# The low part of a weight quarter made by ScalarE and an adding transfer, and high products ahead of low ones

## The chip, the cores and the metric

The program runs on one core of a Trainium2 chip. The metric is the device time of one execution in microseconds (us), from the first instruction to the last. Five engines work side by side, each through its own instruction queue in order: TensorE (PE: matmuls, with its weight loads shown as PEld), VectorE (DVE), ScalarE (ACT), GpSimd (POOL) and SyncE (SP, which here only issues transfers). Transfers from the chip's memory (DRAM) to the on-chip buffer run on 16 DMA engines and are issued from the queues of SP, ACT or POOL.

## The reference

One backbone layer over 256 latent tokens and 256 context tokens of width 2048, in float32:

```python
h  = modulate(rmsnorm(x, norm1_w), sh1, sc1);  hc = the same for ctx
rw, cv, z, ab, gt = split(h @ w_in);  rw_c, ... = split(hc @ w_in)
out_a = prefix_scan(rwkv7_scan, ...)       # 16 heads of 64, two directions, context first
out_b = prefix_scan(gdn_chunked, ...)      # 8 heads of 128, two directions, context first
y = (sigmoid(g_a) * (o_a @ p_a) + sigmoid(g_b) * (o_b @ p_b)) @ w_out
x = x + gt1 * y
x = x + gt2 * swiglu(modulate(rmsnorm(x, norm2_w), sh2, sc2), w_gate_up, w_down)
return rmsnorm(x, final_norm_w)
```

Every large product (`h @ w_in`, the merges, `w_out`, the FFN) has to be close to float32.

## The kernel before

**Split products.** TensorE is given float32 numbers rounded to a shorter form (F32R). A weight block is therefore split: `hi = round(raw)`, `lo = raw - hi`; the activations are kept split in the same way (`HX`, `HC`: a high and a low tile of the latent and of the context tokens). A product is three matmuls per 128 rows of weights: hi with high, hi with low, lo with high.

**Blocks and quarters.** A block of `w_in` is 2048 by 128, that is 16 slices of 128 by 128. It is loaded, split and used in four quarters of four slices (`CG = 4`; a quarter is 128 x 512 numbers, 256 KB), numbered q = 0 to 3. A block for both token groups (what = k, v, K, V) takes 24 matmuls a quarter, two-sided; one for the latent tokens alone (r, Q, and g, the 40 gate blocks) takes 12, one-sided. There are 86 blocks of `w_in` in this part, 31 two-sided and 55 one-sided. Blocks of the merge matrices `pa` and `pb` have at most two quarters.

**What a quarter passes through.** `fetch` takes a raw buffer from the ring `raws` (three buffers at first, up to six later) and has SP issue the load. `cast` waits for the landing, takes a slot of the ring `his` and has ScalarE write `hi`; takes a slot of `los` and has VectorE write `lo`; gives the raw buffer back; and marks the quarter as cast. `products` runs the matmuls and gives the slots of `his` and `los` back after the quarter's last one. Both rings have four slots, so a quarter's cast can start only when the quarter four before it, the same q of the block before, is used up.

**The order of the work.** From about 100 us to 1330 us of the span a planner (`Weave`) weaves many generators together: the products, which fill TensorE whenever nothing of higher rank is ready, and the chains of the two scans (`prepare`, `grams`, `inverse`, `scan`, then `features`, `decays`, `head_grams`, `head_inverse`, `head_scan`). Each yields operations with an estimated cost (`LAT` holds the constants); the planner picks whichever can start first and so writes out a fixed order for each of TensorE, VectorE, ScalarE and GpSimd. On the chip every engine keeps that order, whatever the real times are. SP issues the loads as the plan asks for them. All operations of the woven part have line 164 in the profile, where a helper records them (SP's loads have line 175, preloads of activation tables line 154). After it come the last merges and `w_out` (L1861, L1862), and the FFN (L426, L427, L436 to L438), which use other code.

Of the kernel before, what the change touches and what calls it, by code (L numbers as in the profile page):

```python
# [11 lines left out]
F32 = mybir.dt.float32  # L12
F32R = mybir.dt.float32r
AF = mybir.ActivationFunctionType
ALU = mybir.AluOpType
# [3 lines left out]
P = 128  # L19
D = 2048  # L20
KT = D // P
T = 256
# [5 lines left out]
NHELD, NB = 10, 10  # L28
GATES_A, GATES_B = ((36,0,0,0,0,0,0,0),(0,0,0,0,0,4,0,0))

LAT = dict(dma=3.1, v=1.0, s=1.0, hop=dict(e=0.215, v=0.135, s=0.15, g=0.1), slack=0.1, own=0.09, grp=32, crank=-1, cg=4, into=0.14, back=0.2, cross=0.14, stay=0.0, gpace=1.6)
LNEXP = "natural_log_exp_and_others"
SIGM = "sigmoid_and_others"
UNIT = 64 * 64 + 64
# [78 lines left out]
class Lane:  # L113
# [36 lines left out]
    def __getattr__(self, name):  # L150

        def op(out, *a, **k):
            if name == "preload_act_table_set":
                return Op(self, 1.2, lambda: self.engine.preload_act_table_set(out))
            if name == "dma_start":
                return Op(self, 0.6 if self.each > 0.002 else 0.06, lambda: self.engine.dma_start(out, *a))
            mode = base = None
            if name == "transpose" and len(a) == 2:
                cost, mode = 0.109, "full"
            elif name == "matmul":  # L160
                cost, mode = self.product(out, a)
            else:
                cost, base = self.cost(name, out, a, k), (out.offset // out.ap[0][0], out.shape[0])
            return Op(self, cost, lambda: getattr(self.engine, name)(out, *a, **k), mode, base)  # L164
        return op
# [163 lines left out]
def emit(ctx: ExitStack, tc, A, out, dbg=None):  # L329
# [4 lines left out]
    weave = Weave()  # L334
    dq = Loads(Q)
    e, v, s, g = (Lane(x, fixed, each, LAT["own"], LAT["hop"][n]) for x, fixed, each, n in
                  ((E, 0.0, 0.0, "e"), (V, 0.07, 0.00104, "v"), (S, 0.06, 0.0009, "s"), (G, 0.06, 0.0022, "g")))
# [137 lines left out]
    with tc.tile_pool(name="p0", bufs=1) as p0, \  # L475
# [12 lines left out]
        low = [pst(pi, "pi"), pst(pmm, "mm"), pst(psq, "s"), pst(psq, "s"), pst(pmm, "mm"), pst(pa, "pa")]  # L488
# [23 lines left out]
        ps = pst(pa, "pa")  # L512
# [71 lines left out]
        for part in range(NE + 1):  # L584
            if part < NE:
                ps = pst(pmm, "mm")
            for c in range(4):
# [4 lines left out]
                if c == 0 and part < NE:  # L592
                    w = low_split(part)
# [197 lines left out]
    CG = LAT['cg']  # L791
# [5 lines left out]
    raws, his, los = quarters("wraw", 3, F32), Ring(quarters("whi", 2, F32R)), Ring(quarters("wlo", 2, F32R))  # L797
# [366 lines left out]
    def cast(parts, i):  # L1164

        for q, part in enumerate(parts):
            n = part.shape[1]
            yield "asked", i, q
            raw, at = landed.pop((i, q))
            yield max(0.0, at - weave.now)  # L1170
            hi = yield his
            yield s.copy(hi[:, :n], raw[:, :n])
            lo = yield los
            yield v.tensor_sub(lo[:, :n], raw[:, :n], hi[:, :n].bitcast(F32))
            raws.put(raw)
            casts[i, q] = hi, lo
            weave.ready("cast", i, q)

    def weights(parts, i):
        weave.add(LAT['crank'], fetch(parts, i))  # L1180
# [74 lines left out]
    def products():  # L1255
# [53 lines left out]
        while todo or ahead:  # L1309
            ask(1)  # L1310
            if not ahead:
                yield 0.5
                continue
            what, p, need = ahead.pop(0)
            ask(NQ)
            if need is not None:
                yield need
            if what == "l":
                yield "cast", i, 0
                hi, lo = casts.pop((i, 0))  # L1320
                yield "part", NGH - 1
                for j in range(p, min(p + CG, NHELD)):
                    for n, (w, part) in enumerate(((hi, 0), (hi, 1), (lo, 0))):
                        yield e.matmul(held[j // 2][:, T * (j % 2):T * (j % 2) + T], w[:, j - p], OB[part][:, NGH - 1, :],
                                       start=False, stop=j % 2 == 1 and n == 2)
                    if j % 2:
                        weave.add(150, second_merge(j - 1, 2, held[j // 2], homes[j // 2]))
                his.put(hi)
                los.put(lo)
                i += 1  # L1330
                continue
            if what != "b":
                ps = yield mmb
            elif p % 2 == 0:
                if p >= 6:
                    yield "inv", NGH - 1
                held.append((yield homes[p // 2]))
            if what in "bf":
                nk = NGH - (what == "b")
                half = p % 2 if what == "b" else 0  # L1340
                for k in range(nk):
                    if k % CG == 0:
                        ask(NQ, k == CG)
                        yield "cast", i, k // CG
                        hi, lo = casts.pop((i, k // CG))
                    yield "part", k
                    for j, (w, part) in enumerate(((hi, 0), (hi, 1), (lo, 0))):
                        yield e.matmul((held[-1] if what == "b" else ps)[:, T * half:T * half + T], w[:, k % CG], OB[part][:, k, :],
                                       start=k + j + half == 0, stop=what == "f" and k == nk - 1 and j == 2)
                    if k in (CG - 1, nk - 1):  # L1350
                        his.put(hi)
                        los.put(lo)
                i += 1
                if what == "f":
                    weave.add(150, second_merge(p, 1, ps))
                continue
            sides = ((0, OA),) if what == "p" else ((0, HX), (1, HC))[:1 + (what in "kvKV")]
            nk = OA[0].shape[1] if what == "p" else KT
            for k in range(nk):
                if k % CG == 0:  # L1360
                    ask(NQ, k == nk - CG)
                    yield "cast", i, k // CG
                    hi, lo = casts.pop((i, k // CG))
                for j, (w, part) in enumerate(((hi, 0), (hi, 1), (lo, 0))):
                    for a, X in sides:
                        yield e.matmul(ps[:, T * a:T * a + T], w[:, k % CG], X[part][:, k, :], start=k + j + a == 0,
                                       stop=k == nk - 1 and j == 2 and a == len(sides) - 1)
                if k % CG == CG - 1:
                    his.put(hi)
                    los.put(lo)  # L1370
            i += 1
            if what not in NPARTS and not any(x[0] not in NPARTS for x in todo + ahead):
                weave.ready("sides")
            if what == "g":
                weave.add(150, gate_out(rs, p, ps))
            elif what == "p":
                weave.add(150, first_merge(p, ps, p == KT - 1))
            else:
                (hd if what in "KVQ" else pr)[p][what + "ps"] = ps
                weave.ready(what + "gemm", p)  # L1380
# [713 lines left out]
```

## Time and profile before

| what | us |
|---|---|
| median of 3 runs | 2189.1 (2182.12 to 2189.5) |
| the profiled execution, its own time | 2182.99 |
| its span, first to last instruction | 2181.2 |
| PE busy in the span | 2104.2 |
| DVE busy in the span | 1551.6 |
| ACT busy in the span | 1119.0 |
| POOL busy in the span | 19.3 |

A busy PE counts the whole modelled time of a matmul, and matmuls overlap in a pipeline, so a short wait between two of them can hide in its share. In the rows, "x" is a count, "<-" in a group is output from inputs, and "<-" behind an idle time names what ended it. The granted TensorE clock was 0.989 of full speed on the mean.

### The profile page before, as it was taken

Reading aid. Unit: us, or ns where it says so; the run is one execution under the profiler, and the core shown is the slowest. Engines: PE = TensorE matmul, PEld = TensorE weight load, DVE = VectorE, ACT = ScalarE, POOL = GpSimd, SP = SyncE. Lnnn points to the kernel's source line nnn. Section 1 sums busy time; section 2 is a strip of 40 time slices with the busy share of each in tenths; the row PEclk is TensorE's granted clock in tenths of the full one; section 3 lists DMA queues with packets and bytes.
Section 4 is the critical chain, followed back from the end, with each engine's and each line's share of the span. In section 5 each row is a group of like instructions: output and inputs, shape, how many; then the busy total and the mean of one; then the engine's idle time right before and its main releaser. Section 6 shows DMA issues by size and latency. Waiting matters only on the chain.

```text
span 2181.2 us, 59117 instructions
## 1 busy us (share of the span) xinstructions
PE 2104.2 (96%) x24536; PEld 1973.0 (90%) x24536; DVE 1551.6 (71%) x3305; ACT 1119.0 (51%) x2210; POOL 19.3 (1%) x55
## 2 busy tenths in 40 slices
PE   7999999999999999999999998999999999999997
PEld 4987698888898898998989988999999999999997
DVE  4466599889889976898998777865666665554554
ACT  3246654555555556565565664644444444444443
POOL 0000000000000000000000000000000000000000
PEclk9999999999999999999999999999999999999999
DMA  9966756645565564665653745946777776566665
GB/s 385 410 168 198 228 140 180 188 141 154 164 162 154 159 168 142 188 194 169 173 160 105 218 151 178 306 161 216 242 244 239 242 239 209 195 191 194 196 194 163
DMA packets 276813, 431.14 MB, mean 198 GB/s; under 512 B 119872, under 2 KB 137664, under 8 KB 272192
## 3 DMA queue, kind: packets, MB, share of 16 engines
q1 hardware_dynamic: 262720, 402.19, 60.0%
q10 hardware_dynamic: 13824, 25.17, 3.6%
q8 instruction: 192, 3.15, 0.6%
q14 instruction: 77, 0.63, 0.1%
HBM read 401.50 MB, written 25.77 MB: 196 GB/s over the span
## 4 chain that ended last, share of the span: by engine, by line
PE 80%; DVE 7%; DMA 7%; ACT 3%; issue 2%; SPq 1%; DVEq 0%; ACTq 0%
PE mm L164 27%; PE mm L438 12%; PE mm L437 12%; PE mm L436 12%; PE s L164 6%; PE pa L164 5%; PE pi L164 3%; DVE arena L164 2%; DMA wraw<-w 2%; DVE wlo L164 1%; DMA wraw<-ada_rest 1%; PE mm L529 1%; PE s L579 1%; PE mm L579 1%; ACT whi L164 1%
## 5 line engine op out<-in xcount | busy, mean ns | idle before, releaser
L427 DVE TENSOR_TENSOR wlo<-wraw,whi 128x1024 fp32r<-128x1024 f32 (+1 forms) x264 | 315.0, 1193 | 292.6 <-ACT whi L426 292.4
L426 ACT CAST whi<-wraw 128x1024 fp32r<-128x1024 f32 (+1 forms) x264 | 270.6, 1025 | 386.6 <-PE mm L437 341.7
L164 PE MATMUL mm<-hxh,wlo 128*128 128x256 f32 x1376 | 399.5, 290 | 7.0 <-DVE wlo L164 6.4
L164 PE MATMUL mm<-hxh,whi 128*128 128x256 f32 x1376 | 397.2, 289 | 2.8 <-ACT whi L164 1.8
L164 PE MATMUL mm<-hxl,whi 128*128 128x256 f32 x1376 | 395.7, 288 | 0.0
L438 PE MATMUL mm<-hfh,wlo 128*128 128x256 f32 x1344 | 371.7, 277 | 0.6 <-DVE wlo L427 0.6
L436 PE MATMUL mm<-hfh,whi 128*128 128x256 f32 x1344 | 371.0, 276 | 0.0
L437 PE MATMUL mm<-hfl,whi 128*128 128x256 f32 x1344 | 371.0, 276 | 0.0
L164 ACT CAST whi<-wraw 128x512 fp32r<-128x512 f32 (+1 forms) x399 | 243.1, 615 | 206.1 <-PE mm L164 93.5
L164 DVE TENSOR_TENSOR wlo<-wraw,whi 128x512 fp32r<-128x512 f32 (+1 forms) x399 | 270.4, 680 | 86.0 <-ACT whi L164 82.7
L164 PEld LDWEIGHTS mm<-hxh,wlo 128*128 128x128 f32 x1376 | 260.7, 189 | 17.9 <-DVE wlo L164 9.8
L164 PEld LDWEIGHTS mm<-hxh,whi 128*128 128x128 f32 x1376 | 260.7, 189 | 10.9 <-issue 4.1
L164 PEld LDWEIGHTS mm<-hxl,whi 128*128 128x128 f32 x1376 | 261.1, 190 | 6.5 <-issue 4.1
L438 PEld LDWEIGHTS mm<-hfh,wlo 128*128 128x128 f32 x1344 | 252.3, 188 | 1.1 <-DVE wlo L427 1.0
L437 PEld LDWEIGHTS mm<-hfl,whi 128*128 128x128 f32 x1344 | 252.3, 188 | 0.0
L436 PEld LDWEIGHTS mm<-hfh,whi 128*128 128x128 f32 x1344 | 252.3, 188 | 0.0
L164 PE MATMUL mm<-hch,wlo 128*128 128x256 f32 x496 | 142.3, 287 | 0.0
L164 PE MATMUL mm<-hcl,whi 128*128 128x256 f32 x496 | 142.2, 287 | 0.1
L438 PE MATMUL mm<-za,wlo 128*128 128x256 f32 x512 | 141.4, 276 | 0.1
L436 PE MATMUL mm<-za,whi 128*128 128x256 f32 x512 | 141.5, 276 | 0.0
L437 PE MATMUL mm<-za,whi 128*128 128x256 f32 x512 | 141.3, 276 | 0.0
L164 PE MATMUL mm<-hch,whi 128*128 128x256 f32 x496 | 140.9, 284 | 0.0
(417 smaller groups left out, 4519.8 us busy)
## 6 DMA issues: line engine op xcount, KB each, us to landing
wraw<-w SPq DMA_DIRECT2D x344, 256.0 KB, 3.3
wraw<-wgu SPq DMA_DIRECT2D x168, 512.0 KB, 4.7
aw<-ada_first SPq DMA_DIRECT2D x32, 1024.0 KB, 10.3
wraw<-wdn SPq DMA_DIRECT2D x64, 448.0 KB, 3.7
wraw<-ada_rest SPq DMA_DIRECT2D x96, 256.0 KB, 3.3
aw<-ada_rest SPq DMA_DIRECT2D x48, 512.0 KB, 4.3
wraw<-wout SPq DMA_DIRECT2D x64, 256.0 KB, 5.9
aw<-ada_gt ACTq DMA_DIRECT2D x64, 256.0 KB, 5.2
```

The source lines that it names most:

```text
L164: return Op(self, cost, lambda: getattr(self.engine, name)(out, *a, **k), mode, base)
L426: S.copy(hi[:, c, :M], raw[:, c, :M])
L427: V.tensor_sub(lo[:, c, :M], raw[:, c, :M], hi[:, c, :M].bitcast(F32))
L436: E.matmul(ps, hi, Xh[:, k, :n], start=first and i == 0, stop=False)
L437: E.matmul(ps, hi, Xl[:, k, :n], start=False, stop=False)
L438: E.matmul(ps, lo, Xh[:, k, :n], start=False, stop=last and i == len(wt) - 1)
L529: E.matmul(ps[32 * g:32 * g + 32, 0:P], ckr[:, k].rearrange("p a b -> p (a b)"), aws[e, c][:, i, g], start=k == 0, stop=k == KT - 1)
L579: E.matmul(ps[:m, T * a:T * a + T], w_, X[:, 2 * e + k, :], start=e == k == i == 0, stop=e == NE - 1 and k == 1 and i == len(todo) - 1)
```

## The change

In the woven part, for the blocks with four quarters:

- For the last quarter of each block (q = 3) the subtraction on VectorE goes. ScalarE, behind its cast, writes minus the high part into the low slot, and a transfer issued from GpSimd's queue reads the raw weights from DRAM a second time and adds them there. The raw buffer goes back as soon as the cast is issued.
- For every quarter of these blocks TensorE now runs the eight (one-sided) or sixteen (two-sided) products with `hi` first and then the four or eight with `lo`. The low part has a mark of its own ("low"), and only the low products wait for it. Products of `pb` keep their order and wait for both marks.
- The planner's costs get a time for the adding transfer (`acc=4.0`).

```diff
-LAT = dict(dma=3.1, v=1.0, s=1.0, ... gpace=1.6)
+LAT = dict(dma=3.1, v=1.0, s=1.0, ... gpace=1.6, acc=4.0, share=lambda i, q: q == 3)
...
-                return Op(self, 0.6 if self.each > 0.002 else 0.06, lambda: self.engine.dma_start(out, *a))
+                return Op(self, 0.6 if self.each > 0.002 else 0.06, lambda: self.engine.dma_start(out, *a, **k))
...
             yield s.copy(hi[:, :n], raw[:, :n])
             lo = yield los
-            yield v.tensor_sub(lo[:, :n], raw[:, :n], hi[:, :n].bitcast(F32))
-            raws.put(raw)
             casts[i, q] = hi, lo
-            weave.ready("cast", i, q)
+            if len(part.shape) == 3 and part.ap[-2][0] == P and LAT["share"](i, q):
+                raws.put(raw)
+                weave.ready("cast", i, q)
+                weave.add(LAT['crank'], low_part(part, lo[:, :n], hi[:, :n].bitcast(F32), i, q))
+            else:
+                weave.ready("cast", i, q)
+                yield v.tensor_sub(lo[:, :n], raw[:, :n], hi[:, :n].bitcast(F32))
+                raws.put(raw)
+                weave.ready("low", i, q)
+
+    def low_part(part, lo, hi, i, q):
+
+        yield s.activation(lo, hi, AF.Copy, scale=-1.0)
+        yield g.dma_start(lo, part, accum_op=ALU.add)
+        yield LAT["acc"]
+        weave.ready("low", i, q)
...
-                for j, (w, part) in enumerate(((hi, 0), (hi, 1), (lo, 0))):
+                for j, part in enumerate((0, 1)):
                     for a, X in sides:
-                        yield e.matmul(ps[:, T * a:T * a + T], w[:, k % CG], X[part][:, k, :], start=k + j + a == 0,
-                                       stop=k == nk - 1 and j == 2 and a == len(sides) - 1)
+                        yield e.matmul(ps[:, T * a:T * a + T], hi[:, k % CG], X[part][:, k, :], start=k + j + a == 0, stop=False)
                 if k % CG == CG - 1:
+                    yield "low", i, k // CG
+                    for kk in range(k - CG + 1, k + 1):
+                        for a, X in sides:
+                            yield e.matmul(ps[:, T * a:T * a + T], lo[:, kk % CG], X[0][:, kk, :], start=False,
+                                           stop=kk == nk - 1 and a == len(sides) - 1)
                     his.put(hi)
                     los.put(lo)
```

Because the planner's costs and marks change, it writes a new order for the whole woven part. Three places of it follow; a row is line, operation, output and inputs, shape, and a count.

The start of a quarter of a gate block on TensorE, before: each slice has its low product right behind its two high ones, and the quarter's first low product waits for VectorE.

```order
L164 MATMUL mm<-hxh,whi 128x256 [waits Activation_49]
L164 MATMUL mm<-hxl,whi 128x256
L164 MATMUL mm<-hxh,wlo 128x256 [waits DVE_49]
L164 MATMUL mm<-hxh,whi 128x256
L164 MATMUL mm<-hxl,whi 128x256
```

The end of a last quarter (q = 3) of such a block on TensorE, and the start of the block behind it, now:

```order
L164 MATMUL mm<-hxh,whi 128x256
L164 MATMUL mm<-hxl,whi 128x256
L164 MATMUL mm<-hxh,wlo 128x256 [waits DMASW2_49]
L164 MATMUL mm<-hxh,wlo 128x256 x3
L164 MATMUL mm<-hxh,whi 128x256 [waits Activation_49]
L164 MATMUL mm<-hch,whi 128x256
```

The four low products stand together behind the eight high ones and wait for a transfer of GpSimd's queue (DMASW) instead of VectorE; nothing else stands between the high and the low products here.

On GpSimd, in the second head pair (`prepare`: a memset of `ei`, the copy and the sum of `bon`, and the memsets of the next inverse), before:

```order
L896 MEMSET arena 128x8
L928 COPY bon<-arena 128x256
L900 MEMSET arena 128x8
L930 TENSOR_TENSOR bon<-bon,arena 128x256
L164 MEMSET arena 128x256
```

The same place now:

```order
L896 MEMSET arena 128x8
L156 DMA wlo<-w 128x512
L928 COPY bon<-arena 128x256
L900 MEMSET arena 128x8
L156 DMA wlo<-w 128x512
L930 TENSOR_TENSOR bon<-bon,arena 128x256
L156 DMA wlo<-w 128x512 x2
L164 MEMSET arena 128x256
```

Transfers (86 in all) now stand between and behind GpSimd's own instructions, some of which wait for VectorE.

On ScalarE, where the gates are turned into sigmoids (`gts<-gts`) near the end of the woven part and a head's readout (`arena<-s,C`: logarithm, then exponential) comes by, before:

```order
L164 ACTIVATE gts<-gts 128x512
L164 COPY PA<-mm 128x256
L164 CAST whi<-wraw 128x512
L154 ACT_TABLE_LOAD
L164 CAST whi<-wraw 128x512
L164 ACTIVATE arena<-arena 128x256
L164 COPY PA<-mm 128x256
L164 CAST whi<-wraw 128x512
L164 ACTIVATE arena<-s,C 128x256
```

And now:

```order
L164 ACT_TABLE_LOAD
L164 ACTIVATE arena<-s,C 128x256
L164 ACT_TABLE_LOAD
L164 ACTIVATE gts<-gts 128x512
L164 ACT_TABLE_LOAD
L164 ACTIVATE arena<-arena 128x256
L164 COPY PA<-mm 128x256
L164 ACT_TABLE_LOAD
L164 ACTIVATE gts<-gts 128x512
```

The readout has moved ahead of the last sigmoids and in between them, with four table loads around it. Over the whole program ScalarE has 39 table loads in its order where it had 34.

More of the change, by code (lines that the diff above doesn't have):

```diff
@@ L29 @@
 GATES_A, GATES_B = ((36,0,0,0,0,0,0,0),(0,0,0,0,0,4,0,0))
-LAT = dict(dma=3.1, v=1.0, s=1.0, hop=dict(e=0.215, v=0.135, s=0.15, g=0.1), slack=0.1, own=0.09, grp=32, crank=-1, cg=4, into=0.14, back=0.2, cross=0.14, stay=0.0, gpace=1.6)
+LAT = dict(dma=3.1, v=1.0, s=1.0, hop=dict(e=0.215, v=0.135, s=0.15, g=0.1), slack=0.1, own=0.09, grp=32, crank=-1, cg=4, into=0.14, back=0.2, cross=0.14, stay=0.0, gpace=1.6, acc=4.0, share=lambda i, q: q == 3)
 LNEXP = "natural_log_exp_and_others"
@@ L1319, in products @@
                 yield "cast", i, 0
+                yield "low", i, 0
                 hi, lo = casts.pop((i, 0))
@@ L1363, in products @@
                     hi, lo = casts.pop((i, k // CG))
-                for j, (w, part) in enumerate(((hi, 0), (hi, 1), (lo, 0))):
+                for j, part in enumerate((0, 1)):
                     for a, X in sides:
-                        yield e.matmul(ps[:, T * a:T * a + T], w[:, k % CG], X[part][:, k, :], start=k + j + a == 0,
-                                       stop=k == nk - 1 and j == 2 and a == len(sides) - 1)
+                        yield e.matmul(ps[:, T * a:T * a + T], hi[:, k % CG], X[part][:, k, :], start=k + j + a == 0, stop=False)
                 if k % CG == CG - 1:
+                    yield "low", i, k // CG
+                    for kk in range(k - CG + 1, k + 1):
+                        for a, X in sides:
+                            yield e.matmul(ps[:, T * a:T * a + T], lo[:, kk % CG], X[0][:, kk, :], start=False,
+                                           stop=kk == nk - 1 and a == len(sides) - 1)
                     his.put(hi)
```

## The prediction

> **What bounds the kernel now.** I read the page first, then the windows, the groups, the waits, and single stretches of the timeline and of the chain.
>
> The page's span, busy times and chain:
>
> ```profile
> span 2181.2 us, 59117 instructions
> PE 2104.2 (96%) x24536; PEld 1973.0 (90%) x24536; DVE 1551.6 (71%) x3305; ACT 1119.0 (51%) x2210; POOL 19.3 (1%) x55
> PE 80%; DVE 7%; DMA 7%; ACT 3%; issue 2%; SPq 1%; DVEq 0%; ACTq 0%
> ```
>
> TensorE carries four fifths of the chain that ended last; VectorE is on it for 7%, about 153 us, ScalarE for 3%, about 65 us. The windows show where the rest lies: first the woven part as a whole, then 100 us of it, then 100 us of the FFN (columns: window, its length, then busy us and count for PE, PEld, DVE, ACT, POOL, the granted clock, the DMA share, GB/s).
>
> ```profile
> 100.00:1330.00 1230.00, 1188.15 (x16140) 1079.44 (x16128) 1004.50 (x2481) 701.62 (x1628) 18.88 (x50) 0.99 0.59 171
> 300.00:400.00 100.00, 96.36 (x1386) 89.11 (x1384) 88.98 (x199) 54.47 (x136) 3.60 (x10) 1.00 0.63 176
> 1500.00:1600.00 100.00, 100.00 (x884) 100.00 (x883) 61.69 (x92) 44.19 (x55) 0.00 (x0) 1.00 0.76 244
> ```
>
> In the FFN TensorE is never idle. In the woven part it is idle for 1230 - 1188.15 = 41.9 us, and VectorE is busy for 82% of it, 89% in the quoted stretch. Only this part is touched. The groups give the prices:
>
> ```profile
> L164 PE MATMUL mm<-hxh,wlo 128*128 128x256 f32 x1376 | 399.5, 290 | 7.0 <-DVE wlo L164 6.4
> L438 PE MATMUL mm<-hfh,wlo 128*128 128x256 f32 x1344 | 371.7, 277 | 0.6 <-DVE wlo L427 0.6
> L164 DVE TENSOR_TENSOR wlo<-wraw,whi 128x512 fp32r<-128x512 f32 (+1 forms) x399 | 270.4, 680 | 86.0 <-ACT whi L164 82.7
> L164 ACT CAST whi<-wraw 128x512 fp32r<-128x512 f32 (+1 forms) x399 | 243.1, 615 | 206.1 <-PE mm L164 93.5
> L164 ACT ACTIVATE arena<-arena 128x512 f32<-128x512 f32 (+2 forms) x108 | 62.3, 585 | 24.2 <-DVE arena L164 19.7 <-issue 3.4
> L164 ACT ACT_TABLE_LOAD x14 | 18.0, 1283 | 0.2
> 1269.87 8.09 PE mm L164 x71
> ```
>
> The same product takes 290 ns in the woven part and 277 ns in the FFN; the 13 ns are short waits hidden in the pipeline. The last row, of the chain, is the pace of products that wait for nothing: 8.09 us for 71, or 0.114 us each. So a one-sided quarter (12 products) is 1.37 us of TensorE, a two-sided one 2.74. The waits that the change touches:
>
> ```profile
> PE mm L164 <- DVE wlo L164: 6.4, 13, 1.5
> PEld mm L164 <- DVE wlo L164: 9.8, 16, 1.7
> ACT whi L164 <- PE mm L164: 93.5, 66, 4.9
> SPq L175 <- DVE wlo L164: 226.4, 166, 6.9
> ACT whi L164 <- DMA wraw<-w: 68.5, 48, 3.2
> ```
>
> TensorE visibly waits for a low part for 6.4 us only (9.8 at its weight loads, the same waits seen one step earlier). Casts wait for a slot (ScalarE on TensorE, 93.5 us) more than for a load (68.5 us).
>
> **The change, part by part.**
>
> *The subtractions that go.* 86 x 0.680 = 58.5 us of VectorE, 5.8% of its 1004.5 us there. Only the time when VectorE is on the path counts. Most of the 153 us of chain on VectorE lies in the woven part; I take 130, and 5.8% of that is 7.5 us. The ends are 0 and 41.9 us (all idle time of TensorE); I take 8, because the idle time is spread over many releasers.
>
> *High products first.* The first low product moves from the third to the ninth place of a one-sided quarter, 6 x 0.114 = 0.7 us later, and from the fifth to the seventeenth of a two-sided one, 1.4 us later. The longest wait of 13 was 1.5 us, so nearly all 6.4 us go. Where the supply of casts is the limit the wait only moves to the next high part; hidden waits go too. I take 6, between 0 and 16 (6.4 + 9.8).
>
> *Raw buffers back earlier.* A quarter of SP's 226.4 us of waits for a subtraction are of last quarters, and their buffer comes back about 1 us sooner. A load that comes sooner helps where a cast waited for it, a quarter of 68.5 us at most; TensorE mostly did not wait for that. I take 2, between 0 and 17.
>
> *The adding transfer.* Nothing in the trace adds on its way, and nothing is issued by GpSimd's queue. The nearest rows (KB each, us from issue to landing) and the slots:
>
> ```profile
> wraw<-w SPq DMA_DIRECT2D x344, 256.0 KB, 3.3
> wraw<-wgu SPq DMA_DIRECT2D x168, 512.0 KB, 4.7
> sgd__1597<-lo ACTq DMA_DIRECT2D x32, 256.0 KB, 4.1
> 405.76 0.62 ACT L164 CAST whi<-wraw 128x512 fp32r<-128x512 f32 x1
> 406.41 0.69 DVE L164 TENSOR_TENSOR wlo<-wraw,whi 128x512 fp32r<-128x512 f32 x1 [0.38 <-PE pa L164]
> 1199.26 0.62 ACT L164 CAST whi<-wraw 128x512 fp32r<-128x512 f32 x1 [1.21 <-PE mm L164]
> 1201.08 0.62 ACT L164 CAST whi<-wraw 128x512 fp32r<-128x512 f32 x1 [1.20 <-PE mm L164]
> ```
>
> It must at least read 256 KB as a plain load does, 3.3 us; it reads the low tile as well, 512 KB together, 4.7 us; were it a load and then a write one behind the other, 3.3 + 4.1 = 7.4. I take 4.7, whose byte count it shares. The low part is then ready at: slot free, cast 0.62, minus high 0.6 (between the 585 and 615 ns rows), handovers (406.38 to 406.41 is 0.03) 0.1, transfer 4.7, and some 0.4 behind other work on ScalarE, which is busy 57% of the time (701.62 of 1230): 6.4 us. The ends are 5.0 and 9.1.
>
> Against it stands the time from the release of the slot (the last low product of the block before) to the first low product of this last quarter. With nothing between products that is three quarters and eight products: 44 x 0.114 = 5.0 us one-sided, 10.0 two-sided. Two-sided blocks are covered to the upper end. One-sided ones: the two cast rows at 1199.26 and 1201.08 are a stretch of Q blocks whose casts wait for slots, 1.82 us a quarter, so 3 x 1.82 + 0.9 = 6.4 us; and over the whole part the products of all 86 blocks (55 x 5.5 + 31 x 10.9 = 640 us) fill about 1100 us, so the mean is 5.0 x 1.7 = 8.6 us. A quarter of the 55, the gate blocks with little between them, I put below 6.4, short by 0.5 us on the mean: 14 x 0.5 = 7 us of waiting. At the lower end it is 0. At the upper end (9.1) some 40 blocks are short by 1.9 us: 76 us.
>
> The Trainium skill (DMA: Bandwidth & Descriptors, section "Anatomy of one DMA — SWDGE (gpsimd) path") gives a transfer issued from GpSimd as about 2.0 us plus the bytes at 436 GB/s, which is an estimate of 2.6 us for 256 KB without the adding. No run here shows such a transfer, and SP's plain load took 3.3 us. By that page the low part would be ready in 4.3 us, the 7 us would be 0 and the sum -10, or 2173, still inside the forecast's own range.
>
> *ScalarE.* 86 x 0.6 = 52 us for minus high, and five more table loads (39 against 34 in the order) at 1.283: 6.4 us, together 58 us on 701.6, 8.3%. Cover: ScalarE's 43% of idle time. Of its 65 us on the chain some 45 lie in the woven part; 8.3% is 4 us. Four of the loads fall into the stretch of sigmoids, in front of casts that feed TensorE; the four slots hold 5.5 us of one-sided products, so I add only 1. Total 5, between 0 and 58.
>
> *DMA.* 22.5 MB more are read and as much is read back from the low tiles, in a part whose engines are 59% busy; q1's 402 MB take 60% of the whole span, so 45 MB are about 7% of it, or 12% of the woven part. Engines stay under 75%; loads that meet an adding transfer land a little later. I take 1, between 0 and 10.
>
> *GpSimd's queue.* 86 issues on an engine that is busy 18.9 of 1230 us: 0, as long as its own instructions do not hold the transfers up (a rival).
>
> Sum: -8 - 6 - 2 + 7 + 5 + 1 = -3 us. Against the profiled execution (2182.99, span 2181.2) that is 2180. The median of the runs shown is 6.1 us above that execution and the lowest run 0.9 below; the 2180 is on the execution's own scale.
>
> **The rivals.** About 0.5%, 11 us, is what a measurement of this kernel can tell from no change; the bounds are then 2172 and 2194.
>
> *VectorE sets the pace more than its share of the chain says.* For: 89% busy in the quoted stretch, and the 13 ns hidden in each of some 5,600 products are 73 us that the idle time does not show. Against: TensorE's waits name many releasers. If a third of the 58.5 us comes back beside the other gains, -20 - 8 + 7 + 5 + 1 = -15: 2168; to 2155 at best.
>
> *The adding transfer is slow (the other side).* Place: TensorE's first low product of the last quarter in one-sided blocks. It decides from about 6.4 us behind the release of the slot; at the upper end, 9.1 us, 76 us are lost instead of 7, and the sum is +66: 2249; halfway, at 7.7, some 30 blocks short by 1 us give +20: 2203. For: nothing in the trace shows such a transfer. Against: its bytes are those of a 4.7 us row.
>
> *GpSimd's own instructions hold the transfers.* In the order a transfer stands behind nearly each of the 16 `bon` instructions, which wait for VectorE:
>
> ```profile
> L930 POOL TENSOR_TENSOR bon<-bon,arena 128x256 f32<-128x256 f32 x8 | 7.7, 957 | 167.3 <-DVE arena L164 167.3
> L928 POOL COPY bon<-arena 128x256 f32<-128x256 f32 x8 | 5.5, 690 | 430.2 <-DVE arena L164 327.0 <-DVE Y L164 103.2
> ```
>
> How late VectorE is at that point no row shows; if the 16 transfers come 2 us late and half of them run out of cover, +16: 2196. Against: the planner emits these next to the VectorE work that they wait for. A rule of the Trainium skill stands beside this (SBUF — State Buffer, section "Who interferes with whom"): descriptor generation on GpSimd is locked out while VectorE runs in a two-port mode. No run here shows that.
>
> *ScalarE becomes the engine waited for.* If its 58 us lie on the path for a quarter rather than a twelfth: +10, 2190.
>
> *The change does not do what it says.* The subtractions do go from VectorE's order, so this is only that nothing is limited by them: then -8 + 13, 2188.
>
> **How the numbers follow.** The forecast (2172 to 2190 around 2180, most terms small and of both signs): 0.42. VectorE sets the pace: 0.26. Slow transfer: 0.13, most of it near 2203. GpSimd's queue: 0.07. ScalarE: 0.07. Nothing limited: 0.05. Faster by over 0.5%: the 0.26 and 0.06 from the forecast's low end, 0.32. Slower: the 0.13, the 0.07, half of ScalarE and 0.03 of the forecast's terms at their upper ends, 0.27. The rest, 0.41, is no change. The range that leaves at most 2 in 10 out reaches from the best of VectorE's case, 2155, to past the halfway point of the slow transfer, 2215; the likeliest case alone is 2172 to 2190.
>
> **What would show it.** In the trace after: VectorE's subtractions of L164 down from 399 to 313 and its busy time by 58 us; 86 ACTIVATE of the low tile on ScalarE at about 0.6 us; 86 issues of 256 KB from POOL's queue with a median of 4 to 5 us to landing (a median of 6 or more speaks for the slow transfer); TensorE's waits for VectorE's low tile near 0, and new waits for a transfer of about 7 us in gate blocks; ScalarE with 19 table loads on L164. I am wrong if the landing is far from 4.7 us, or if TensorE's products drop from 290 to nearly 277 ns, which would mean that the hidden waits were VectorE's.

## The result, and the profile after

The changed kernel takes 2268.4 us (median of 5 runs, 2256.2 to 2271.0) against 2185.6 us before (5 runs): a ratio of 1.036, interval 1.034 to 1.039. It is slower, and lies outside the predicted range of 2155 to 2215.

The profiled execution after has a span of 2254.0 us, 72.8 us more than before. The page's span and busy times, the row of HBM, and three rows of transfers (KB each, median us from issue to landing):

```profile
span 2254.0 us, 59240 instructions
PE 2119.7 (94%) x24536; PEld 1987.5 (88%) x24536; DVE 1506.9 (67%) x3219; ACT 1176.3 (52%) x2301; POOL 97.0 (4%) x141
...
HBM read 424.05 MB, written 25.77 MB: 200 GB/s over the span
...
wraw<-w SPq DMA_DIRECT2D x344, 256.0 KB, 3.6
...
aw<-ada_rest SPq DMA_DIRECT2D x48, 512.0 KB, 5.2
wlo<-w POOLq DMA_DIRECT2D x86, 256.0 KB, 5.3
```

VectorE's busy time fell by 45 us, ScalarE's rose by 57, GpSimd's by 78 (86 issues). HBM reads rose by 22.55 MB, 86 times 256 KB. The adding transfers land in 5.3 us at the median, and SP's loads of the same size in 3.6 instead of 3.3.

The groups of the same products and operations as before, and the new ones:

```profile
L164 PE MATMUL mm<-hxh,wlo 128*128 128x256 f32 x1376 | 288.4, 293 | 33.6 <-DMA wlo<-w 32.9
...
L164 DVE TENSOR_TENSOR wlo<-wraw,whi 128x512 fp32r<-128x512 f32 (+1 forms) x313 | 212.1, 680 | 77.5 <-ACT whi L164 69.5
```

```profile
L164 ACT ACTIVATE wlo<-whi 128x512 fp32r<-128x512 f32 x86 | 54.3, 632 | 15.3 <-PE mm L164 11.5 <-issue 1.5 <-ACT whi L164 0.2
L164 ACT ACT_TABLE_LOAD x19 | 24.4, 1283 | 1.7 <-DMA arena<-gts__1615 1.4
```

The low products wait 32.9 us for the transfer, where they had waited 6.4 us for VectorE. That is not half of the 72.8 us. The window of 100 to 1330 us, the same stretch as in the prediction:

```profile
100.00:1330.00 1230.00, 1142.75 (x15393) 1035.52 (x15392) 915.54 (x2297) 716.77 (x1635) 96.57 (x136) 0.98 0.67 180
100.00:1395.00 1295.00, 1199.50 (x16070) 1089.86 (x16069) 955.58 (x2388) 756.41 (x1715) 96.57 (x136) 0.97 0.66 179
```

TensorE is idle for 87 us of the first window instead of 42, and issues 15393 matmuls in it instead of 16140; the DMA engines are busy for 67% instead of 59%. It needs 65 us more, the second window, to get nearly as far (16070). Over the whole span TensorE's idle time rose by 57.3 us (77.0 to 134.3) and its busy time by 15.5 for the same 24536 matmuls, so a part of the loss shows as longer matmuls and not as idle time. The other losses are spread thinly. VectorE's wait for the loads of `ada_rest` grew, while the casts' wait for `wraw` fell (68.5 us in 48 before). First VectorE's row before, then both after:

```profile
DVE wraw L164 <- DMA wraw<-ada_rest: 14.4, 11, 3.5
...
DVE wraw L164 <- DMA wraw<-ada_rest: 47.9, 22, 5.8
ACT whi L164 <- DMA wraw<-w: 41.9, 32, 4.5
```

No row tells which part of the change costs what; the experiments do.

### The profile page after: what moved, and what is told of

The parts are those of the page before. It is cut to its first block, busy times and chain, and to the rows that moved or that the text cites. A ratio compares the mean times of both kernels' runs of the same rounds, so it can differ in the third digit from the quotient of the medians.

```text
span 2254.0 us, 59240 instructions
## 1 busy us (share of the span) xinstructions
PE 2119.7 (94%) x24536; PEld 1987.5 (88%) x24536; DVE 1506.9 (67%) x3219; ACT 1176.3 (52%) x2301; POOL 97.0 (4%) x141
## 3 DMA queue, kind: packets, MB, share of 16 engines
q0 software_dynamic: 12384, 22.55, 6.0%
## 5 line engine op out<-in xcount | busy, mean ns | idle before, releaser
L164 PE MATMUL mm<-hxh,whi 128*128 128x256 f32 x1376 | 374.9, 292 | 3.2 <-ACT whi L164 2.7
L164 PE MATMUL mm<-hxl,whi 128*128 128x256 f32 x1376 | 374.9, 291 | 0.0
L164 PE MATMUL mm<-hxh,wlo 128*128 128x256 f32 x1376 | 288.4, 293 | 33.6 <-DMA wlo<-w 32.9
L164 PEld LDWEIGHTS mm<-hxh,whi 128*128 128x128 f32 x1376 | 265.4, 193 | 10.8 <-issue 3.9
L164 DVE TENSOR_TENSOR wlo<-wraw,whi 128x512 fp32r<-128x512 f32 (+1 forms) x313 | 212.1, 680 | 77.5 <-ACT whi L164 69.5
L164 PEld LDWEIGHTS mm<-hxh,wlo 128*128 128x128 f32 x1376 | 220.9, 194 | 44.2 <-DMA wlo<-w 37.5
L164 DVE TENSOR_TENSOR arena<-arena 128x512 f32<-128x512 f32 (+17 forms) x522 | 120.4, 232 | 25.0 <-DMA arena<-scr 10.9
```

## The experiments

Each time is a median, and the ratio is to the kernel before on the same chip, with its 95% interval. Differences between runs are taken between ratios, times 2186 us.

### Taking the change apart, its order kept

Three kernels keep the changed order on every engine but for a few neighbouring rows, and take away one thing after the other.

**1. No wait for the transfer.** In the 86 quarters the low products read the high part, so these quarters' low part is left out of the output. The same edit stands in every run that starts from this one.

```diff
+                    low = hi if (i, k // CG) in minus_ else lo
...
-  yield e.matmul(ps[:, ...], lo[:, kk % CG], X[0][:, kk, :], ...)
+  yield e.matmul(ps[:, ...], low[:, kk % CG], X[0][:, kk, :], ...)
```

> The changed kernel, but in the 86 last quarters the low products read the high part instead of the low one. Minus-high and the adding transfer are still written into the low tile, every engine keeps its order; only TensorE's wait for the transfer is gone (the low part of these quarters is left out of the output). If TensorE loses the time by waiting for the transfer (32.9 us seen at its products, and what follows from each wait on the chains behind it), most of the 73 us of span come back: 2185 to 2205. If the load that the transfers put on the DMA engines, on GpSimd's queue and on ScalarE is the cause, or the new order itself, it stays within 35 us of the changed kernel: 2220 or more.

2245.0 us, 1.028 [1.0251, 1.0309]. The wait and all that followed from it were 0.8% (1.0363 - 1.0280), 18 us with about 9 either way. Three quarters of the loss stay though TensorE waits for no transfer of GpSimd: the first theory, that the wait is nearly all, falls.

**2. No transfer.**

```diff
-        yield g.dma_start(lo, part, accum_op=ALU.add)
+        move = g.dma_start(lo, part, accum_op=ALU.add)
+        move.call = lambda: None
+        yield move
```

> As the run without the wait, and the 86 adding transfers are not issued either (minus-high is still written by ScalarE). Against that run it shows what the transfers cost as load alone: by DMA traffic (22.5 MB read, 22.5 MB read back, the loads of ada_rest waited for 47.9 us instead of 14.4) and by 75 us of issue on GpSimd with its memsets and copies behind it. If that load matters, 15 to 35 us less than the run without the wait; if the wait alone mattered, within 8 us of it.

2204.9 us, 1.0093 [1.0061, 1.0126]. The transfers cost 1.9% (1.0280 - 1.0093), 41 us with about 10 either way, as load alone, more than the range that was expected. Rows of plain transfers of this run:

```profile
wraw<-w SPq DMA_DIRECT2D x344, 256.0 KB, 3.3
...
aw<-ada_rest SPq DMA_DIRECT2D x48, 512.0 KB, 4.5
...
scr<-arena SPq DMA_DIRECT2D x32, 128.0 KB, 2.8
```

and of the run without the wait:

```profile
wraw<-w SPq DMA_DIRECT2D x344, 256.0 KB, 3.5
...
aw<-ada_rest SPq DMA_DIRECT2D x48, 512.0 KB, 5.2
...
scr<-arena SPq DMA_DIRECT2D x32, 128.0 KB, 3.4
```

A median moves by only 0.2 to 0.7 us, but every kind of transfer in these rows lands later, and what counts are the loads that somebody waits for. ScalarE's and VectorE's waits for plain loads, first without transfers, then with them:

```profile
ACT whi L164 <- DMA wraw<-w: 35.1, 27, 3.4
DVE wraw L164 <- DMA wraw<-ada_rest: 32.6, 22, 4.0
```

```profile
ACT whi L164 <- DMA wraw<-w: 58.1, 41, 4.7
DVE wraw L164 <- DMA wraw<-ada_rest: 50.8, 28, 5.1
```

These two alone are 41 us more; they lie on two engines, so they are not a sum of lost time. They suggest where the transfers are felt, but such rows also move without them (14.4 us for `ada_rest` before, and 26.7 in a run below that takes no longer). On TensorE the spans of the two profiled executions differ by 35.0 us: 18.1 more of idle time (98.0 to 116.1) and 16.9 more of busy time (2106.8 to 2123.7) for the same matmuls. The mean granted clock of these two is 0.989 and 0.982; 0.007 of 2107 us is an estimate of 15 us, so nearly all of the busy time's share can be the clock.

**3. The order alone.** ScalarE's minus-high goes too.

```diff
-        yield s.activation(lo, hi, AF.Copy, scale=-1.0)
+        neg = s.activation(lo, hi, AF.Copy, scale=-1.0)
+        neg.call = lambda: None
+        yield neg
```

> As the run without transfers, and ScalarE's 86 minus-high activations are gone too: what is left is the changed kernel's order with nothing in place of the 86 subtractions. If ScalarE's 54 us and the table loads around them matter, 10 us or more below the run without transfers; if not, within 5 us. If the order that the planner makes for the change is bad in itself (the theory of the order), this run is still above 2210; if the order is as good as the one before, it is at 2170 to 2190, with 58 us less work on VectorE than the kernel before.

2199.9 us, 1.0068 [1.004, 1.0096]. Minus-high is worth 0.25%, 5 us, which these intervals do not tell from nothing. What is left, with no work at all in place of 86 subtractions, is still 0.7% slower than before, 15 us: between the two ranges that were expected.

So the 79 us are: 15 the new order (less what the missing subtractions gave back), 5 ScalarE, 41 the load of the transfers, 18 the wait for them.

**4. What the missing subtractions are worth.** The kernel before, in its own order, without them.

```diff
+            if len(part.shape) == 3 and part.ap[-2][0] == P and q == 3:
+                sub.call = lambda: None
+                lo = lo, hi
```

> The kernel before, in its own order, with the 86 subtractions of the last quarters not issued (their low products read the high part; the low part of these quarters is left out). It shows what 58 us of VectorE are worth where nothing is put in their place. If VectorE sets the pace (the rival of the prediction), 15 to 30 us less than before: 2158 to 2173. If TensorE and the planned order set it, as the run with the changed order and nothing in place of the subtractions (2200) suggests: within 8 us of before, 2178 to 2190.

2187.6 us, 1.0007 [0.9992, 1.0022]: nothing. The page of this run, to set beside the 1551.6 us of VectorE before, and the group of the high products with the latent's high tile:

```profile
span 2183.6 us, 58959 instructions
...
PE 2102.9 (96%) x24536; PEld 1975.3 (90%) x24536; DVE 1502.0 (69%) x3219; ACT 1116.7 (51%) x2210; POOL 18.4 (1%) x55
...
L164 PE MATMUL mm<-hxh,whi 128*128 128x256 f32 x1720 | 452.5, 289 | 3.4 <-ACT whi L164 2.4 <-ACT arena L164 1.0
```

VectorE does 49.6 us less, and the span does not follow. If the missing subtractions are worth as little in the changed order, the 15 us of the run above are all the order's.

### What of the transfers costs

Four kernels start from the run without the wait (1.028 with the transfers, 1.0093 without).

**5. GpSimd's own instructions elsewhere.** The memsets of `ei` and the `bon` instructions go to VectorE.

```diff
-                G.memset(ei[:, :, 0:1], 1.0)
+                V.memset(ei[:, :, 0:1], 1.0)
...
-                G.tensor_copy(kb, kd[:, 0:T])
+                V.tensor_copy(kb, kd[:, 0:T])
```

> As the run without the wait (2245 us, against 2205 without transfers), but GpSimd's own 16 one-column memsets and 16 `bon` instructions in the woven part run on VectorE, so that GpSimd only issues the 86 adding transfers. If the transfers cost their 40 us because GpSimd's own instructions and the transfers hold each other up in one queue, most of it comes back: 2205 to 2220. If it is the traffic on the DMA engines, it stays at 2240 to 2255 (VectorE has some 7 us more to do).

2249.9 us, 1.030 [1.0275, 1.0324]: nothing comes back. GpSimd's own instructions between the transfers are not the cause.

**6. The same read on ScalarE's queue, to DRAM.**

```diff
+        move.call = lambda: S.dma_start(next(away), part)
```

> As the run without the wait, but each adding transfer is replaced by a plain copy of the same 256 KB from the weights to a buffer in DRAM, issued on ScalarE's queue right behind minus-high. Traffic of 22.5 MB read and 22.5 MB written stays, GpSimd issues nothing and nothing writes the low tile behind ScalarE. If traffic on the DMA engines is the cost: 2230 to 2250. If GpSimd's way of issuing (0.87 us each, descriptors written first) or the writing into the low tiles is: 2205 to 2215.

2236.7 us, 1.0237 [1.0213, 1.026]: 31 us, with about 9 either way, without GpSimd and without a write into the low tile. So a like amount of traffic can cost most of the 41 us without GpSimd's way of issuing. It is not the same traffic, as these copies also write 22.55 MB to DRAM.

**7. Copied, not added.**

```diff
-        yield g.dma_start(lo, part, accum_op=ALU.add)
+        yield g.dma_start(lo, part)
```

> As the run without the wait, but GpSimd's transfers copy the raw weights into the low tile without adding to it. If the adding (a second read of 256 KB in each) is what loads the DMA engines, it comes down to 2215 to 2225; if it is the issue on GpSimd or the first read, it stays within 8 us of 2245. The landing shows the price of adding: 5.3 us median with it; 3.6 as a plain load if adding is the difference.

2225.7 us, 1.0172 [1.0146, 1.0199]: 17 us of the 41, with about 9 either way. The landing came down to 4.1 us, not to the 3.6 of a plain load of SP.

**8. A quarter of the bytes.**

```diff
-        yield g.dma_start(lo, part, accum_op=ALU.add)
+        yield g.dma_start(lo[:, :1], part[:, :1], accum_op=ALU.add)
```

> As the run without the wait, but each adding transfer moves a quarter of its bytes (64 KB, one of the four 128x128 pieces; the rest of the low part is left as minus-high). The count of transfers and of issues on GpSimd stays at 86. If bytes on the DMA engines are the cost, three quarters of the 40 us come back: 2210 to 2220; if the count of issues on GpSimd is, it stays at 2235 to 2250.

2213.4 us, 1.0128 [1.0108, 1.0147]: 8 us of the 41, with about 8 either way, so hardly told from nothing. The count of issues is the same, and each still takes GpSimd 0.87 us. The rows of GpSimd's queue (packets, MB, share of 16 engines' span) and of its transfers: added whole in the run without the wait, then copied, then a quarter added:

```profile
wlo<-w POOLq DMA_DIRECT2D x86, 256.0 KB, 5.3
...
q0 software_dynamic: 12384, 22.55, 6.0%
```

```profile
wlo<-w POOLq DMA_DIRECT2D x86, 256.0 KB, 4.1
...
q0 software_dynamic: 12384, 22.55, 3.7%
```

```profile
wlo<-w POOLq DMA_DIRECT2D x86, 64.0 KB, 4.1
...
q0 software_dynamic: 12384, 5.64, 2.1%
```

Of these three, 2.1% of the engines' time cost 8 us, 3.7% cost 17 and 6.0% cost 41: the cost grows with the time that the packets take. Whether it grows faster than that time, these intervals of 8 to 10 us do not show. Adding makes the same bytes take 1.6 times the engines' time. The copies to DRAM may not lie on this line: they raised the share of ScalarE's queue (q10) from 3.5% to 6.8% and cost 31 us; whether that is for the 22.55 MB that they write stays open.

**9. The same traffic in the order before.** Nobody waits for these copies.

```diff
             lo = yield los
+            if len(part.shape) == 3 and part.ap[-2][0] == P and q == 3:
+                S.dma_start(next(away), part)
```

> The kernel before, complete and in its own order, with 86 plain copies of 256 KB more, from the weights of each last quarter to a buffer in DRAM, issued on ScalarE's queue behind the quarter's cast; nobody waits for them. If traffic on the DMA engines by itself costs some 0.7 us for each of the 45 MB, whatever the order (the run with the same copies in the changed order lost 32 us by them), 2210 to 2220. If it cost that only in the changed order, which has lost its slack, within 10 us of before.

2210.5 us, 1.0111 [1.0078, 1.0145]: 24 us in the order of the kernel before, against 31 in the changed one. That the traffic costs is no property of the new order. One more thing could cost here and in the run with the copies above: each issue stands in ScalarE's queue (ns, min/median/max):

```profile
L1176 ACTq DMA_DIRECT2D away<-w x86: 497/498/598, 133.4 to 1232.3; - x86
```

Together these are 43 us of ScalarE's queue, but each is issued behind a cast that takes 0.62 us itself, and the trace names only 3 instructions of ScalarE that waited for such an issue, 9.8 us in all. So some of the 24 us can be the issuing; no run here takes it apart.

### The order

**10. High products first, nothing else.**

```diff
-share=lambda i, q: q == 3
+share=lambda i, q: False
```

> The changed kernel with no quarter shared: VectorE subtracts everywhere as before, and the high products of each quarter run ahead of its low products (the planner orders for that). If high products first is harmless, 2175 to 2195 as the kernel before; if the new order of products costs time (slots for high and low parts are held longer and come back together), above 2200.

2216.4 us, 1.0137 [1.0116, 1.0157]: 30 us, where the prediction had a gain of 6. The waits for VectorE's low part did go (6.4 us before):

```profile
ACT whi L164 <- DMA wraw<-w: 54.9, 37, 3.5
...
PE mm L164 <- ACT whi L164: 6.6, 10, 1.2
...
PE mm L164 <- DVE wlo L164: 0.6, 2, 0.4
```

The wait moved to the next high part: 6.6 us for ScalarE's cast, as long as the one it replaced.

**11. The high slot back at once.**

```diff
                 if k % CG == CG - 1:
+                    his.put(hi)
                     yield "low", i, k // CG
...
-                    his.put(hi)
                     los.put(lo)
```

> As the run with high products first and all subtractions on VectorE (2216), but the slot of the high part goes back as soon as the last high product is written, ahead of the low products. If high products first costs its 28 us because the slots of the high part are held through the low products and casts wait for them, most of it comes back: 2190 to 2200. If it is the pattern of products or the planner's luck with it, 2205 to 2225.

2209.3 us, 1.0103 [1.0065, 1.0141]. Some 7 us came back, and the interval overlaps that of the run above; most of the cost stays. Slots held longer are not the main part of it.

**12 and 13. Other orders for nothing.** Two numbers of the planner, changed in the kernel before.

```diff
-slack=0.1,
+slack=0.11,
```

> The kernel before with one number of the planner changed that no instruction depends on: its allowance for a handover between engines, 0.11 us instead of 0.10. The same instructions come in another order. If the order of the kernel before is a lucky one among many that are alike by the planner's account, this one costs 10 to 30 us more: 2197 to 2217, and the 11 to 28 us of the runs without transfers are no more than that. If orders that differ so little take the same time, 2180 to 2192.

2192.7 us, 1.0033 [1.0015, 1.0051].

```diff
-LAT = dict(dma=3.1,
+LAT = dict(dma=3.2,
```

> The kernel before with another number of the planner changed that no instruction depends on: its latency of a load, 3.2 us instead of 3.1. A second draw of an order that is as good by the planner's account. By the first draw (+7 us), 2185 to 2200; if the spread of such orders is as wide as the 28 us of high products first, it can be above 2205.

2195.0 us, 1.0040 [1.0022, 1.0057]. Two orders that the planner holds to be as good cost 7 and 9 us: less than the 10 to 30 expected, but both in the same direction. So a part of the 15 and of the 30 us may be no more than another order in place of this one. What the other 20 us or so of high products first are is not settled.

**14. Low products in their old places**, with the transfers:

```diff
-                for j, part in enumerate((0, 1)):
...
+                for j, (w, part) in enumerate(((hi, 0), (hi, 1), (lo, 0))):
+                    if j == 2:
+                        yield "low", i, k // CG
```

> The changed kernel with the products of a quarter in the old pattern (two high products, then the low one, for each piece), so that the first low product waits for the transfer from the third place on. If running the high products first gives the transfer time that it needs, this costs 86 waits of some 0.7 to 1.4 us more: 2290 to 2350. If the cost of the pattern itself (28 us) outweighs that, 2240 to 2265.

2262.5 us, 1.0356 [1.031, 1.0402], the same as the changed kernel. Its wait for the transfer:

```profile
PE mm L164 <- DMA wlo<-w: 62.4, 35, 6.1
```

The new pattern saves 29.5 us of that wait (32.9 against 62.4) and saves no time, which fits its price of 30 us by itself; as this run has another order too, more than that is not shown.

### Two ways to mend it

**15. A planner that knows the landing.**

```diff
-acc=4.0
+acc=6.5
```

> The changed kernel, complete, with the planner told that a low part comes 6.5 us behind the issue of its transfer instead of 4.0 (the traces show 5.3 to 5.4 from issue to landing and 0.87 of issue ahead). If the waits of TensorE for the transfer (23 us by the run without the wait) come from planning them too early, they fall to under 10 us and the time to 2235 to 2255. If the transfer is late because ScalarE and GpSimd come late to it, or there is nothing else to put in between, it stays at 2260 to 2275.

2275.1 us, 1.0401 [1.037, 1.0431]: no better, and at the upper end of the second range that was expected. The wait is halved,

```profile
PE mm L164 <- DMA wlo<-w: 17.1, 9, 6.6
```

and the time is lost elsewhere: TensorE's idle time in its profiled execution is 132.5 us, about as much as after (134.3), and its busy time 2140.0 against 2119.7, at a mean granted clock of 0.970, against 0.983 after and 0.989 before.

**16. GpSimd subtracts.** The kernel before, the 86 subtractions on GpSimd.

```diff
+            x = g if len(part.shape) == 3 and part.ap[-2][0] == P and q == 3 else v
-            yield v.tensor_sub(lo[:, :n], raw[:, :n], hi[:, :n].bitcast(F32))
+            yield x.tensor_sub(lo[:, :n], raw[:, :n], hi[:, :n].bitcast(F32))
```

> The kernel before with the 86 subtractions of the last quarters on GpSimd instead of VectorE: no transfer, no work for ScalarE, the products in the old pattern. If a freed VectorE is worth something, 2165 to 2180; if nothing waits for VectorE, 2180 to 2195; if GpSimd is too slow for a low part that is due 1 us after its high part (it took 957 ns for an addition half that size), its products wait: above 2200.

2217.7 us, 1.0139 [1.0104, 1.0175].

```profile
L164 PE MATMUL mm<-hxh,wlo 128*128 128x256 f32 x1376 | 401.7, 292 | 7.0 <-DVE wlo L164 4.0 <-POOL wlo L164 2.8
...
L164 POOL TENSOR_TENSOR wlo<-wraw,whi 128x512 fp32r<-128x512 f32 x86 | 119.4, 1389 | 943.3 <-ACT whi L164 819.3 <-PE pa L164 42.6 <-DMA aw<-ada_rest 23.3
```

A subtraction takes GpSimd 1389 ns, where VectorE takes 680, and TensorE waits only 2.8 us for it. The planner wrote another order here too; the rest of the 30 us was not taken apart. No version here beats the kernel before.

## Why the prediction was wrong

Forecast and measured sum are 82 us apart (-3 and 79). By the runs above, 40 of these lie in the term for DMA, 31 in the three gains (-16 together, where the order cost 15), 11 in the wait for the adding transfer and none in ScalarE.

**DMA, the step that failed.** It took +1 (0 to 10) because the engines would stay under 75%. They do (0.67 in the window), and the extra engine time was about as foretold (6.0% of the span measured, about 7% forecast), and yet the load of the transfers costs 41 us. So the step from the engines' share to a price was wrong, not the amount of traffic. The mean share did not show how late a single load comes: the woven part lives on loads of 3 to 5 us with three to six raw buffers, and the waits for them had their own rows in the profile before (68.5 us of casts for `wraw`, 14.4 of VectorE for `ada_rest`). That the 41 us come by way of these loads is argued from the waits and landings of experiment 2; no run shows it by itself.

**High products first.** Forecast -6 (-16 to 0). Measured +30 alone. The prediction itself said that the wait may only move to the next high part; that happened, and a new order of the whole woven part came with it. That order was given no term; two orders changed for nothing cost 7 and 9 us. In the changed order with nothing in place of the subtractions the loss was 15 us; why the one is 30 and the other 15 stays open.

**The adding transfer's wait.** Forecast +7 (0 to 76), measured 18, with 32.9 us visible at the products. The place and the count were about right: TensorE waited 18 times, all in one-sided blocks, where 14 quarters were taken to be short. The length was not: 1.8 us on the mean instead of 0.5. A part of that is the landing, 5.3 us where I took 4.7 from the row with the same byte count. Adding is what makes it so: the plain copy by GpSimd landed in 4.1 us. The Trainium skill (DMA: Bandwidth & Descriptors, section "Anatomy of one DMA — SWDGE (gpsimd) path") gives 2.6 us for this size, as an estimate by its rule; the plain copy beside this kernel's other traffic took 4.1, so here the measurement decides, and the sum of -10 by that page was further off than mine.

**The subtractions.** Forecast -8 (-41.9 to 0), measured between 2 us gained and 5 us lost. The rival "VectorE sets the pace" falls with it. VectorE was 89% busy in the quoted stretch and had 7% of the chain, and still leaving these 58 us out gained nothing: why so little of VectorE's work is due at once was not followed further. The 13 ns by which products are longer in the woven part are not VectorE's either: in the run without the 86 subtractions the mean of the high products is 289 ns, as before. Nor are they waits spread over all products, as the prediction had it: the median of the woven part's products before is 276 ns, as in the FFN, and the mean is raised by the slowest, of up to 685 ns.

**ScalarE and GpSimd.** +5 and 0 were right as far as the runs can tell (5 us; nothing back with GpSimd's own instructions moved). The 19 table loads, the 86 activations at 0.63 us and the count of 313 subtractions came as foretold. VectorE's busy time fell by 45 us, not by 58, so 13 us of other work on it became longer; the runs do not show why. Raw buffers back earlier (-2) was not tried by itself; it is inside the 15 us of the order.

**The rivals.** "The adding transfer is slow" named the right side and a wrong price: it counted only TensorE's wait. None of the rivals had the transfers harming other loads.

## What to carry to other kernels

Traffic that nobody waits for can still cost: 22.55 MB more took 17 to 41 us here while the DMA engines were busy for 62 to 67% on the mean, so a mean share under the limit is no reason to price it at nothing. The waits for loads that the profile already has tell where to look, but no run here turns them into a price; a run with the added transfers alone, in the order as it is, gives a first one. An engine's share of busy time, even of the chain, is no price for taking work from it; leaving the work out in one run, with the order kept, gives that price before anything is built in its place. Where a planner writes the order, any edit brings a new order, and two neutral edits measured beside it give an idea of what a new order costs by itself.

## What the runs showed of the hardware

**Idle times of TensorE of 2 to 3 us can be followed by half the clock.** A stretch of the timeline of the changed kernel (start us, us, what, and in brackets the idle time before it), a last quarter of a one-sided block:

```profile
182.40 0.28 PE L164 MATMUL mm<-hxl,whi 128*128 128x256 f32 x1
185.35 1.22 PE L164 MATMUL mm<-hxh,wlo 128*128 128x256 f32 x4 [2.68 <-DMA wlo<-w]
186.37 0.41 PE L164 MATMUL mm<-hxh,whi 128*128 128x256 f32 x1
186.59 0.41 PE L164 MATMUL mm<-hxl,whi 128*128 128x256 f32 x1
186.80 0.41 PE L164 MATMUL mm<-hxh,whi 128*128 128x256 f32 x1
```

After 2.68 us of waiting for the adding transfer the products start every 0.21 us instead of every 0.114. The windows before, behind it and after that, the clock third from the end:

```profile
178.50:182.00 3.50, 3.50 (x33) 3.50 (x33) 0.00 (x0) 3.44 (x5) 1.00 (x2) 1.00 0.25 83
...
185.50:189.00 3.50, 3.50 (x17) 3.50 (x18) 0.64 (x3) 2.36 (x5) 0.48 (x1) 0.53 0.69 218
189.00:192.40 3.40, 3.40 (x32) 3.40 (x31) 2.80 (x7) 1.96 (x4) 0.38 (x1) 1.00 0.76 149
```

17 products in 3.5 us at a clock of 0.53, where 33 ran before: the 2.68 us of waiting cost some 1.7 us more in the window behind them. Of the nine waits for the transfer of 2.0 us or more in this execution, seven are followed by products at this pace, at once or within 1.3 us; two (2.84 us at 155.6, 2.40 at 214.4) are not. Over several runs the mean granted clock goes with the lost time: 0.989 before and 0.988 without transfers, 0.985 with plain copies, 0.981 with the adding transfers and no wait, 0.979 in the changed kernel (means over the runs of each). It does not in every run: 0.9885 with a quarter of the bytes, 28 us slower than before, and 0.983 with the high slot back at once, 23 us slower. One hundredth of TensorE's 2104 busy us is an estimate of 21 us, a quarter of the whole loss; it is part of the shares that the experiments give, not beside them. The Trainium skill (TensorE: Matmul & The Clock Gate, section "What's actually happening") gives half the clock after an idle window of about 3.4 us and full clock after about as long a busy one. The trace agrees with the half and with the length of the slow stretch; here an idle time of 2.68 us was enough, and 2.00 us at 1254.9.

**Adding costs the DMA engines time without reading more from HBM.** The HBM row after shows 22.55 MB more, the bytes of the weights alone; the packets of the same bytes took 6.0% of the engines' span added and 3.7% copied, and the landing 5.3 against 4.1 us.

**An adding transfer of a quarter of the bytes lands no sooner than a whole plain one from the same queue.** 64 KB added landed in 4.1 us, as 256 KB copied, in as many packets (12384).
